# A hybrid decoder layer on one core: the attention phase laid out by an event loop, and its result sent to the output projection through DRAM

## The chip, the core and the metric

The kernel runs on one core of a Trainium2 chip. The metric is device microseconds for one execution. The engines have these names: PE is TensorE (matmuls and transposes), ACT is ScalarE, DVE is VectorE, POOL is GpSimd, and SP is SyncE, which here does nothing but issue DMAs. Each engine takes its instructions in the order in which they were written into its own queue, and waits at an instruction whose inputs or buffers are not ready.

## What is computed

The kernel is one decoder layer on x of shape (1, 2048, 1024), float32:

```python
h = rms_norm(x, norm1_g)
proj = h @ w_in
o_a = swa_sink_mixer(qa, ka, va, sinks, rel_bias)     # 4 heads, window 128
o_b = s5_mixer(u, ...)                                # state-space scan, 512 wide
o_c = nsa_mixer(qc, kvc, gates, ...)                  # 4 heads, three branches
mixed = concat([rms_norm(o_a, g), rms_norm(o_b, g), rms_norm(o_c, g)])
x = x + mixed @ w_out
hid = relu(rms_norm(x, norm2_g) @ w_up)
x = x + (hid * hid) @ w_down
```

Inside `nsa_mixer` each block of 128 query rows attends in three branches, and the gated sum of the three is the 256-wide row o_c:

```python
o_cmp = softmax(q @ k_cmp + bias) @ v_cmp     # up to 128 compressed keys ("c")
idx   = top_k(sums of p_cmp, 16)              # 64-row key blocks
o_sel = softmax(q @ k[idx] + bias) @ v[idx]   # selected blocks ("s")
o_win = softmax(q @ k[last 512] + bias) @ v   # window ("w")
o = g0 * o_cmp + g1 * o_sel + g2 * o_win
```

The kernel does not gather the selected blocks. It takes logits against all keys up to the diagonal and adds a mask through extra rows of the key and query tiles.

## The kernel before

Every matmul operand is split into a high and a low part, so that one product is three matmuls: `mm3` (L74) issues high by high (L76), high row by low weight (L77) and low row by high weight (L78). The phases follow one another in the program: the input projection, then attention A, the scan's output and the compression merged together, then `phase_mix` (L978), then the up projection and the down projection. This text is about `phase_mix`: attention C for 16 blocks of 128 rows and the output projection of each.

**One block of attention.** `prep` (L1049) loads the block's q, k and v rows into `tc`, makes the doubled rows `qd` on POOL, transposes them on PE (tiles `ptqc`, `ptkc`, L793) and splits them into `qA`/`qB` and the key tiles. For each branch and each of four heads `Attn.logits` (L827) multiplies q with up to 512 keys at a time into a PSUM tile (`pqc`, `pqw`, `pqs`; L843/L844; two buffers). DVE adds the bias and takes the running maximum (L846), and ACT takes the exponential (L851) into the probabilities `slc`, `slw`, `sls`. `Attn.pv` (L854) then goes over the probabilities two key blocks at a time, for a pair of heads. PE transposes four 128 by 128 pieces into a PSUM tile (`ppc`, `ppw`, `pps`; L864; two buffers). ACT casts this tile to the high part (`thc`, `thw`, `ths`; L867), DVE subtracts that from it to get the low part (`tlc`, `tlw`, `tls`; L868), and PE multiplies both with the values (L872) into `poc`, `pow` or `pos`. I call one such tile a probability tile; a run of the phase has 260 of them (32 of c, 84 of w, 144 of s). `Attn.combine` (L876) copies the branch's result (`oT`), transposes it back (`ptoc`, `ptow`, `ptos`, L884), scales it by the gate on DVE (`ot`) and adds it on POOL into `oc` (L888, L891; three buffers).

**The projection of one block.** `finish_steps` (L1191) loads the rows of A and B into `mix`, scales them on POOL, takes ACT's square (L897) and POOL's reciprocal root of `oc`, and writes the scaled `oc` into the last quarter of `mix` (L899). PE transposes `mix` in two halves (`ptx`, L1212), ACT and DVE split them (`mh` L1214, `ml` L1215), and 48 matmuls with 512 columns (`pw`, L76 to L78) form the 128 by 1024 result. DVE adds the input rows `mx` (L1227), ACT squares (L1230) and sends the rows to DRAM. For blocks 0 to 7 the rows are also scaled (L1239), transposed (`pth`, L1247) and stored in `hT`; for the later blocks `mt` reads rows of `hT` back and `block_sums` (L1260) makes differences that go to `sums` in DRAM. The up projection reads `hT` and `sums` as its factors `fx` (L1431) and splits them on ACT (L1345) and DVE (L1346) into `fh` and `fl`; its first matmuls are `pua` (L1499).

**What sets the order.** `phase_mix` makes lists of steps: the probability products of one pair of heads, the logits of the next, the preparation of the next block, and the projection of the block before. `merge` (L68) interleaves them evenly by their numbers of steps. Within this the framework's scheduler may shift instructions by priority. The projection's matmuls are given low priority (`FILL = 500`, and for blocks 13 to 15 the numbers of `ENDS`), so that they fill gaps of PE; the products with the values may lag by `LAG = 30`, and the transposes of `combine` by `LAG_TURN = 10`.

Of the kernel before, what the change touches and what calls it, by code (L numbers as in the profile page):

```python
# [16 lines left out]
P = 128  # L17
D = 1024
# [10 lines left out]
FILL = 500  # L29
ENDS = {13: 1, 14: 1000, 15: 1000}  # L30
LAG = 30
LAG_TURN = 10
# [942 lines left out]
RING = 6  # L975


def phase_mix(tc, C, x, gains, B, cmp, w_out, out_norm_g, g2, pd, oa_d, ob, x1, hT, xs, rr, rh, ss_a, ss_b, r_d, release):  # L978
    nc = tc.nc
    kcA, kcB, vc = cmp  # L980
    with ExitStack() as ctx:
# [9 lines left out]
        A = Attn(tc, C, lp, sm, ps_s, ps_p, ps_o, ps_t, LAG)  # L991
        small = A.small
# [14 lines left out]
        late = {}  # L1007

        def open_late():
# [19 lines left out]
            nc.sync.dma_start(rt, r_d.rearrange("(i p) -> i p", p=P))  # L1029
            pt = late["ps"].tile([P, NT], F32, tag="pw", name="ptr")  # L1030
            nc.tensor.transpose(pt, rt, C["ident"][:NT, :NT])
            rb = fp.tile([P, NT], F32, name="r_b")
            nc.vector.tensor_copy(rb, pt)
            late["ra"], late["rb"] = ra, rb
            for k in range(NK):
                load_wout(k)

        def load_wout(k):
            fp, wh, wl, go = (late[n] for n in ("fp", "wh", "wl", "go"))
            for n in range(2):  # L1040
                sl = slice(512 * n, 512 * n + 512)
                if n == 0:
                    raw_k = fp.tile([P, D], F32, tag="xt", name=f"oraw{k}", bufs=2)
                    nc.sync.dma_start(raw_k, w_out[0, k * P:(k + 1) * P])
                raw = raw_k[:, sl]
                nc.scalar.activation(wh[k][:, sl], raw, AF.Copy, scale=go[:, k:k + 1])
                nc.vector.scalar_tensor_tensor(wl[k][:, sl], raw, go[:, k:k + 1], wh[k][:, sl], op0=ALU.mult, op1=ALU.subtract)

        def prep(i):  # L1049
            tcc = lp.tile([P, 524], F32, tag="tc", name=f"tc{i}", bufs=1)  # L1050
            nc.sync.dma_start(tcc[:, 0:256], pd["b"][i * P:i * P + P, 128:384])
            nc.sync.dma_start(tcc[:, 256:524], pd["c"][i * P:i * P + P, 128:396])
            qd = lp.tile([P, 6, 2, 64], F32, tag="qd", name=f"qdc{i}", bufs=1)
            twice(nc, qd[:, 0:4], tcc[:, 0:256].rearrange("p (h d) -> p h d", d=64), rh[:, i, 0:4])
            twice(nc, qd[:, 4:6], tcc[:, 256:512].rearrange("p (h d) -> p h d", d=P)[:, :, 0:64], rh[:, i, 4:6])
            pt = turn(nc, C, ps_t, qd, 0, 4, f"qc{i}")
            qA = lp.tile([P, 4, P], F32R, tag="qA", name=f"qA{i}")
            qB = q_lo[i % 2]
            split_q(nc, qA, qB, pt, gains[:, 2:3])
            pt = turn(nc, C, ps_t, qd, 4, 2, f"kc{i}")  # L1060
            ks, kw = slice(i * P, i * P + P), slice((i % RING) * P, (i % RING) * P + P)
            split_k(nc, kAs[:, ks], pt[:, 0], gains[:, 4:5])
            split_k(nc, kAw[:, kw], pt[:, 1], gains[:, 5:6])
            nc.vector.tensor_copy(kBs[0:64, ks], kAs[0:64, ks])
            nc.vector.tensor_copy(kBw[0:64, kw], kAw[0:64, kw])
            vw[i] = lp.tile([P, P], F32R, tag="vw", name=f"vw{i}", bufs=6)
            split_v(nc, Vs[:, i], tcc[:, 320:384])
            split_v(nc, vw[i], tcc[:, 448:512])
            gt = small(12, "gt")
            nc.scalar.activation(gt, tcc[:, 512:524], AF.Tanh, scale=0.5)  # L1070
            nc.vector.tensor_scalar(gt, gt, 0.5, 0.5, op0=ALU.mult, op1=ALU.add)
            return qA, qB, gt.rearrange("p (h b) -> p h b", b=3)

        def cmp_steps(i, qA, qB, gt, oc):
            n = 8 * (i + 1)
            box = {}
            nm, den, w = small(4, "nmc"), small(4, "denc"), small(4, "wc")

            box["sl"] = slc

            def slab():
                return slc

            def po():
                if "po" not in box:
                    box["po"] = ps_o.tile([P, 512], F32, tag="po", name=f"poc{i}")
                return box["po"]
            res = []
            for h in range(4):
                res += A.logits(lambda h=h: slab()[:, h], h, qA, qB, [(0, B["cmp"][:, h, 120 - 8 * i:P], [(kcA[:, 0:n], kcB[:, 0:n])])], -NEG, nm, den, f"c{i}")  # L1090

            def recip():
                nc.vector.reciprocal(den, den)
                if i == 0:
                    nc.vector.tensor_scalar(den, den, C["rows31"], None, op0=ALU.mult)
                nc.vector.tensor_tensor(w, den, gt[:, :, 0], op=ALU.mult)
            res.append(recip)

            def select():
                sl = box["sl"]  # L1100
                nb = 2 * (i + 1)
                pn = lp.tile([P, 4, P], F32, tag="qd", name=f"pn{i}", bufs=1)
                pm = late["fp"].tile([P, P], F32, tag="pm", name=f"pm{i}", bufs=1)
                nc.gpsimd.tensor_tensor(pn[:, :, 0:n], sl[:, :, 0:n], den.unsqueeze(2).broadcast_to([P, 4, n]), op=ALU.mult)
                nc.vector.tensor_reduce(pm[:, 0:n], pn[:, :, 0:n].rearrange("p h m -> p m h"), axis=AX.X, op=ALU.add)
                im, s2, m8 = small(32, "im", 1), small(32, "s2", 1), small(8, "m8", 1)
                nc.vector.tensor_reduce(im[:, 0:nb], pm[:, 0:n].rearrange("p (j f) -> p j f", f=4), axis=AX.X, op=ALU.add)
                nc.vector.tensor_tensor(im[:, 1:nb], im[:, 1:nb], pm[:, 3:n - 1:4], op=ALU.add)
                nc.vector.tensor_tensor(im[:, 0:nb], im[:, 0:nb], C["forced"][:, 30 - 2 * i:30 - 2 * i + nb], op=ALU.max)
                nc.vector.memset(im[:, 0:1], 1e4)  # L1110
                nc.vector.max(m8, im[:, 0:nb])
                nc.vector.match_replace(s2[:, 0:nb], m8, im[:, 0:nb], NEG)
                nc.vector.max(m8, s2[:, 0:nb])
                nc.vector.match_replace(s2[:, 0:nb], m8, s2[:, 0:nb], NEG)
                mk = C["mk"]
                nc.vector.tensor_scalar(mk[:, 64:64 + nb], s2[:, 0:nb], NEG, 1.0, op0=ALU.is_equal, op1=ALU.subtract)
                pt = ps_t.tile([P, 4, P], F32, tag="pt", name=f"ptm{i}")
                nc.tensor.transpose(pt[0:96, 0], mk, C["ident"])
                nc.vector.tensor_copy(qB[64:96], pt[64:96, 0:1].broadcast_to([32, 4, P]))
            for pair in range(2):  # L1120
                res += A.pv(lambda pair=pair: po()[:, 256 * pair:256 * pair + 256], lambda pair=pair: [box["sl"][:, 2 * pair], box["sl"][:, 2 * pair + 1]],
                            lambda b: vc, 1, f"c{i}{pair}")
            res.append(lambda: A.combine(po(), w, oc, True, f"c{i}"))
            if i >= 8:
                res.append(select)
            return res

        def units(i, qA, qB, gt, oc):

# [758 lines left out]
```

## Time and profile before

| | us |
| --- | --- |
| median of 3 runs | 2563.53 (2557.38 to 2566.71) |
| the profiled execution, its own time | 2563.24 |
| span of the profiled execution | 2561.4 |
| mean granted clock of PE, share of full | 0.988 |
| PE busy | 2460.4 |
| DVE busy | 1788.2 |
| ACT busy | 1329.7 |
| POOL busy | 1025.0 |

The times run from the start of the span. Attention C begins at about 612 us, when the last work of the state-space branch still runs beside it; from 712 us it runs with the projection alone; the last product with the values ends at 1278 us, and the first matmul of the up projection starts at 1303.2 us. So `phase_mix` takes some 690 us of the 2561. A matmul's record in the trace reaches from its start to its modelled end, and neighbouring records overlap: one with 512 columns is 0.39 us long where the next starts 0.23 us after it. The busy time of PE therefore counts the ends of matmuls as work, and short waits vanish in it. "Dense" in this text means the time that matmuls need when they follow one another without any wait.

### The profile page before, as it was taken

The page shows a single profiled execution, that of the slowest core. Times are in us where ns is not written, and L with a number is a line of the kernel's source. Part 1 is how long each engine was busy: PE and PEld are TensorE (multiplying, and loading weights), DVE is VectorE, ACT ScalarE, POOL GpSimd, SP SyncE. Part 2 cuts the span into 40 slices and gives each one's busy share as a digit, 9 for nine tenths or more (in the row PEclk, how much of TensorE's full clock was granted, in tenths as well). Part 3 has the DMA queues.
Part 4 walks back from the last instruction along what each step waited for, and adds up shares of the span by engine and source line. Part 5 has one row for each costly group of instructions (what it writes and reads, how often), then busy time and mean ns, then how long its engine had stood idle before and what let it go on. Part 6 is the DMA issues. An engine that isn't in the chain of part 4 may idle for free.

```text
span 2561.4 us, 38083 instructions
## 1 busy us (share of the span) xinstructions
PE 2460.4 (96%) x12766; PEld 2065.3 (81%) x12766; DVE 1788.2 (70%) x3496; ACT 1329.7 (52%) x2768; POOL 1025.0 (40%) x1015
## 2 busy tenths in 40 slices
PE   8999998999899999999989999999999999999999
PEld 8899997777778777778768888788887888888887
DVE  7853876754766677788565655655557888888886
ACT  6453546755766665565455554544444444344442
POOL 0000222212333333242366666566545344544447
PEclk9999999999899999999999999999999999999999
DMA  7462326221312112121456667655547534444336
GB/s 233 136 203 82 108 93 177 75 57 52 112 48 71 58 57 83 44 83 41 148 179 200 186 183 228 211 167 146 151 126 256 165 97 133 133 132 128 120 103 197
DMA packets 390261, 333.02 MB, mean 130 GB/s; under 512 B 42247, under 2 KB 353165, under 8 KB 388625
## 3 DMA queue, kind: packets, MB, share of 16 engines
q1 hardware_dynamic: 352880, 304.37, 39.5%
q10 hardware_dynamic: 37184, 26.22, 3.2%
q8 instruction: 101, 1.65, 0.3%
q14 instruction: 96, 0.78, 0.1%
HBM read 218.05 MB, written 112.45 MB: 129 GB/s over the span
## 4 chain that ended last, share of the span: by engine, by line
PE 63%; DVE 4%; ACT 3%; issue 2%; POOL 2%; DMA 2%; SPq 0%; DVEq 0%; POOLq 0%; ACTq 0%
PE pdc L1678 7%; PE pdb L1678 7%; PE pda L1678 7%; PE pub L1499 6%; PE puc L1499 6%; PE pua L1499 6%; PE pdd L1678 3%; PE pud L1499 3%; PE pos L872 2%; PE pps L864 2%; PE pw L76 2%; PE pw L77 2%; PE pw L78 2%; PE pqs L843 1%; DVE sls L846 1%
## 5 line engine op out<-in xcount | busy, mean ns | idle before, releaser
L1345 ACT CAST v<-vr 128x512 fp32r<-128x512 f32 x224 | 139.4, 624 | 303.6 <-DMA vr<-vd 138.5
L1346 DVE TENSOR_TENSOR v<-vr,v 128x512 fp32r<-128x512 f32 x224 | 235.5, 1059 | 78.9 <-ACT v L1345 77.0
L1678 PE MATMUL pdc<-dw,v 128*128 128x512 f32 x768 | 187.5, 393 | 4.3 <-ACT dw L1345 4.3
L1678 PE MATMUL pdb<-dw,v 128*128 128x512 f32 x768 | 184.9, 390 | 0.0
L1678 PE MATMUL pda<-dw,v 128*128 128x512 f32 x768 | 184.5, 389 | 0.0
L1678 PEld LDWEIGHTS pdc<-dw,v 128*128 128x128 f32 x768 | 145.5, 190 | 35.7 <-ACT dw L1345 4.7
L1678 PEld LDWEIGHTS pdb<-dw,v 128*128 128x128 f32 x768 | 144.6, 188 | 30.2
L1678 PEld LDWEIGHTS pda<-dw,v 128*128 128x128 f32 x768 | 144.1, 188 | 30.0
L550 POOL TENSOR_TENSOR t<-Q,E 128x508 f32<-128x508 f32 x16 | 22.0, 1374 | 364.0 <-ACT Q L530 325.8
L1470 POOL TENSOR_TENSOR fs<-ur,ur 128x512 f32<-128x512 f32 x62 | 92.1, 1485 | 160.3 <-DMA ur<-in_w_up 127.5
L1345 ACT CAST uh<-fs 128x512 fp32r<-128x512 f32 x124 | 76.2, 621 | 151.2 <-PE pub L1499 59.7
L1346 DVE TENSOR_TENSOR ul<-fs,uh 128x512 fp32r<-128x512 f32 x124 | 128.1, 1034 | 32.5 <-ACT uh L1345 32.4
L1346 DVE TENSOR_TENSOR ul<-ur,uh 128x512 fp32r<-128x512 f32 x93 | 101.0, 1087 | 48.9 <-ACT uh L1345 43.1
L76 PE MATMUL pw<-wo_h,mh 128*128 128x512 f32 x256 | 110.2, 431 | 4.3 <-DVE ml L1215 2.0
L868 DVE TENSOR_TENSOR tls<-pps,ths 128x512 fp32r<-128x512 f32 (+1 forms) x144 | 92.9, 658 | 29.8 <-ACT ths L867 22.5
L1515 POOL TENSOR_TENSOR ev<-e,e 128x512 f32<-128x512 f32 x64 | 92.2, 1440 | 47.4 <-issue 25.2
L867 ACT CAST ths<-pps 128x512 fp32r<-128x512 f32 (+1 forms) x144 | 79.1, 565 | 57.8 <-PE pps L864 27.5
L1499 PE MATMUL pub<-fh,uh 128*128 128x512 f32 x256 | 102.5, 401 | 2.9 <-DVE e L1508 2.9
L77 PE MATMUL pw<-wo_l,mh 128*128 128x512 f32 x256 | 104.9, 410 | 0.0
L78 PE MATMUL pw<-wo_h,ml 128*128 128x512 f32 x256 | 104.5, 409 | 0.0
L1499 PE MATMUL pub<-fl,uh 128*128 128x512 f32 x256 | 102.0, 398 | 0.1
L1499 PE MATMUL puc<-fh,uh 128*128 128x512 f32 x256 | 101.1, 395 | 0.9 <-DVE eu L1508 0.9
(563 smaller groups left out, 7855.9 us busy)
## 6 DMA issues: line engine op xcount, KB each, us to landing
vr<-vd SPq DMA_DIRECT2D x224, 256.0 KB
vd<-ev SPq DMA_DIRECT2D x128, 256.0 KB
ur<-in_w_up SPq DMA_DIRECT2D x124, 256.0 KB
vd<-e ACTq DMA_DIRECT2D x64, 256.0 KB
dr<-in_w_down SPq DMA_DIRECT2D x32, 512.0 KB
x<-in_x SPq DMA_DIRECT2D x16, 512.0 KB
mx<-in_x SPq DMA_DIRECT2D x16, 512.0 KB
x<-mx ACTq DMA_DIRECT2D x16, 512.0 KB
```

The lines of the kernel that those rows point to most:

```text
L76: nc.tensor.matmul(out, sh, mh, start=first, stop=False)
L77: nc.tensor.matmul(out, sh, ml, start=False, stop=False)
L78: nc.tensor.matmul(out, sl, mh, start=False, stop=last)
L864: nc.tensor.transpose(pt[:, j, hh], sls[hh][:, (b0 + j) * P:(b0 + j + 1) * P], C["ident"])
L867: nc.scalar.copy(th[:, 0:nb], pt[:, 0:nb])
L868: nc.vector.tensor_tensor(tl[:, 0:nb], pt[:, 0:nb], th[:, 0:nb], op=ALU.subtract)
L1345: nc.scalar.copy(dh, src)
L1346: nc.vector.tensor_tensor(dl, src, dh, op=ALU.subtract)
L1470: nc.gpsimd.tensor_tensor(t, x, y, op=op)
L1499: nc.tensor.matmul(bank[b], w[:, k], h[o][:, k], start=first and k == 0 and n == 0, stop=k == HALF - 1 and n == 2, skip_group_check=True)
L1515: nc.gpsimd.tensor_tensor(tile_("v" + o), x, y, op=op)
L1678: nc.tensor.matmul(bank[b, q], x[:, q, j], y[:, j], start=first and j == 0 and n == 0, stop=j == 1 and n == 2, skip_group_check=True)
```

## The change

The constants `FILL`, `ENDS`, `LAG` and `LAG_TURN` go. `phase_mix` is written anew as routines (Python generators), one or more for each stage of each block: `front`, `keys`, `values`, `compressed`, `select`, `attended`, `logits`, `reduced`, `turned`, `split_p`, `products`, `combined`, `finished`, `filled`, `added`, `posted`. A routine yields an event that it waits for, a ring of buffers that it needs a place in, or an operation as (engine, nanoseconds, function). While the program is built, an event loop (`Flow.run`) keeps the time of each engine, picks the operation that could start first, with the routine's rank deciding among equals, writes its instructions, and moves the engine's time on. All of it stands in `tc.manual_schedule()`, so that the order written is the order on the engines. The rank is 100 times the block number plus an offset.

```diff
-FILL = 500
-ENDS = {13: 1, 14: 1000, 15: 1000}
-LAG = 30
-LAG_TURN = 10
+    def start(self, task):
+        e = task.op[0]
+        t = max(task.t + HEARD[e], self.engines[e])
+        return t if task.engine in (None, e) else max(t, task.end + HEARD[e])
+
+    def run(self):
+        while self.ready:
+            task = min(self.ready, key=lambda k: (self.start(k), k.rank, k.number))
+            s, (e, ns, fn) = self.start(task), task.op
+            self.ready.remove(task)
+            fn()
+            self.engines[e] = s + max(ns - EARLY[e], 30)
+            task.engine, task.end = e, s + ns + TOLD[e]
+            self.advance(task, task.end)
...
+def mm_ns(n):
+    return 8 + 0.427 * n
...
+def cast_ns(n):
+    return 197 + 0.72 * n
...
+            yield "ACT", cast_ns(n), lambda: nc.scalar.copy(th[:, 0:nb], pt[:, 0:nb])
...
+            spawn(products(th, tl, hi, lo, nb, b0, nblk, v_of, name, po_of, prev, me, finished), rank - 1)
+            t = yield "DVE", sub_ns(n), lambda: nc.vector.tensor_tensor(tl[:, 0:nb], pt[:, 0:nb], th[:, 0:nb], op=ALU.subtract)
...
+                t = yield "SP", 50, lambda: nc.sync.dma_start(oc_d[i * P:i * P + P], S["oc"].rearrange("p h d -> p (h d)"))
...
+            rank, fill = 100 * i + R_FINISH, 100 * i + (BACKLOG if i < ENDING else R_FINISH)
...
+                nc.sync.dma_start(mix[:, 768:D], oc_d[rows])
...
+            yield "ACT", 630, lambda: nc.scalar.activation(sq, dst, AF.Square, accum_out=ss)
...
+                for m, (a, b) in enumerate(((mh, wh), (mh, wl), (ml, wh))):
+                    t = yield "PE", mm_ns(512), lambda: nc.tensor.matmul(pw[n], a[half][:, j], b[k][:, sl], start=k == 0 and m == 0, stop=k == NK - 1 and m == 2)
...
+BACKLOG = 400
+R_FRONT = -90
+R_CMP = -88
+R_SELECT = -30
+R_LOGITS = -20
+R_FINISH = 190
+ENDING = 14
```

The arithmetic stays. Both programs issue 12522 PE, 3482 DVE, 2501 ACT and 1020 POOL instructions. The one difference in the work is that `oc` of each block now goes to a DRAM tile `oc_d` and comes back into the last quarter of `mix`, in two DMAs of 128 KB per block (SP has 1259 instructions instead of 1227); `oc` has two buffers instead of three, and `mh` and `ml` are split into halves of their own. The transposes `ptx` and `pth` use the PSUM buffer that `combine` and the preparation use, instead of the one of `pw`. Outside `phase_mix` the code is the same.

On PE in the middle of the phase, before: a probability tile's products (`pos`), a transpose of the window branch (`ppw`) and projection matmuls stand singly among each other.

```order
4354 L76 MATMUL pw_10562<-wo_h_7678,mh_10459 128x512
4355 L77 MATMUL pw_10562<-wo_l_7679,mh_10459 128x512
4356 L78 MATMUL pw_10562<-wo_h_7678,ml_10460 128x512
4357 L872 MATMUL pos_11256<-ths_11527,Vs 128x256
4358 L872 MATMUL pos_11256<-tls_11528,Vs 128x256
4359 L76 MATMUL pw_10562<-wo_h_7680,mh_10459 128x512
4360 L864 MATMUL ppw_11589<-c_ident,slw_11444 128x128
4361 L77 MATMUL pw_10562<-wo_l_7681,mh_10459 128x512
4362 L78 MATMUL pw_10562<-wo_h_7680,ml_10460 128x512
4363 L76 MATMUL pw_10562<-wo_h_7682,mh_10459 128x512
4364 L77 MATMUL pw_10562<-wo_l_7683,mh_10459 128x512
4365 L864 MATMUL ppw_11589<-c_ident,slw_11514 128x128
```

On PE at the like place in the changed program, where L1296/L1297 are the logits, L1354 the products, L1321 the transposes of probabilities and L1657 the projection:

```order
4374 L1296 MATMUL pqs_11496<-kAs,qA_10835 128x512
4375 L1297 MATMUL pqs_11496<-kBs,qB_7329 128x512
4376 L1296 MATMUL pqs_11507<-kAs,qA_10835 128x512
4377 L1297 MATMUL pqs_11507<-kBs,qB_7329 128x512
4378 L1354 MATMUL pow_11380<-tlw_11466,vw_8630 128x256
4379 L1354 MATMUL pow_11380<-tlw_11466,vw_9135 128x256
4380 L1321 MATMUL ppw_11510<-c_ident,slw_11267 128x128
4381 L1321 MATMUL ppw_11510<-c_ident,slw_11270 128x128
4382 L1657 MATMUL pw_11369<-wo_h_7598,ml_11321 128x512
4383 L789 MATMUL ptkc_11536<-c_ident,qdc_11304 128x128 x2
4384 L1296 MATMUL pqs_11518<-kAs,qA_10835 128x512
4385 L1297 MATMUL pqs_11518<-kBs,qB_7329 128x512
4386 L1657 MATMUL pw_11369<-wo_h_7600,mh_11320 128x512
```

A tile's instructions now stand together, and a single projection matmul fills a place between them.

On PE at the end of the phase, before: the last products of attention, the back-transposes `ptow`, half of the transposes of block 15's `mix`, and then its projection.

```order
6144 L872 MATMUL pow_15620<-thw_15716,vw_14642 128x256
6145 L872 MATMUL pow_15620<-tlw_15717,vw_14642 128x256
6146 L884 MATMUL ptow_15744<-c_ident,oTw_15742 128x128 x4
6147 L1212 MATMUL ptx_15783<-c_ident,mix_15753 128x128 x2
6148 L76 MATMUL pw_15794<-wo_h_7678,mh_15774 128x512
```

On PE at the end of the phase now: the last projection matmuls of block 14, all eight transposes of block 15's `mix` (`ptx`), and its projection; the last instruction of attention (`ptow`) is row 5946, and what stands between it and row 6050 is projection.

```order
6048 L1657 MATMUL pw_15791<-wo_l_7609,mh_15709 128x512
6049 L1657 MATMUL pw_15791<-wo_h_7608,ml_15710 128x512
6050 L1622 MATMUL ptx_15807<-c_ident,mix_15726 128x128 x4
6051 L1622 MATMUL ptx_15840<-c_ident,mix_15726 128x128 x4
6052 L1657 MATMUL pw_15860<-wo_h_7594,mh_15805 128x512
6053 L1657 MATMUL pw_15860<-wo_l_7595,mh_15805 128x512
6054 L1657 MATMUL pw_15860<-wo_h_7594,ml_15806 128x512
```

In the changed program 148 projection matmuls follow the last instruction of attention, where 48 did before.

On SP at the end of the phase, before: a load of an up factor (`fx<-sums`, row 495) stands ahead of the last load of input rows.

```order
489 L1258 DMA mt_15456<-hT 128x2x128 x4
490 L1198 DMA mix_15753<-oa_d 128x256
491 L1431 DMA fx_15917<-hT 128x2048
492 L1265 DMA sums<-mt_15456 128x2x128 x4
493 L1199 DMA mix_15753<-ob 128x512
494 L1458 DMA ur_15925<-in_w_up 128x4x128
495 L1431 DMA fx_15919<-sums 128x2048
496 L1201 DMA mx_15756<-in_x 128x1024
```

On SP at the end of the phase now: the writes to `sums` of blocks 13 and 14 (rows 539 and 542), and behind them the loads of factors.

```order
536 L1597 DMA mix_15726<-oc_d 128x256
537 L1638 DMA mx_15721<-in_x 128x1024
538 L1715 DMA mt_15741<-hT 128x2x128 x4
539 L1720 DMA sums<-mt_15741 128x2x128 x4
540 L1638 DMA mx_15837<-in_x 128x1024
541 L1715 DMA mt_15857<-hT 128x2x128 x4
542 L1720 DMA sums<-mt_15857 128x2x128 x4
543 L1852 DMA fx_16003<-sums 128x2048
544 L1852 DMA fx_16053<-sums 128x2048
```

The buffers of `mt` and `mx` are the same two (`xt`), so that `mt` of block 14 (row 541) waits until an earlier block's rows have left theirs.

More of the change, by code (lines that the diff above doesn't have):

```diff
@@ L975, with __init__ @@
 RING = 6
-def phase_mix(tc, C, x, gains, B, cmp, w_out, out_norm_g, g2, pd, oa_d, ob, x1, hT, xs, rr, rh, ss_a, ss_b, r_d, release):
+EARLY = {"PE": 0, "ACT": 98, "DVE": 78, "POOL": 43, "SP": 0}
+TOLD = {"PE": 177, "ACT": 9, "DVE": 12, "POOL": 10, "SP": 0}
+HEARD = {"PE": 103, "ACT": 22, "DVE": 22, "POOL": 68, "SP": 30}
+class Event:
+    def __init__(self):
+        self.time, self.waiting = None, []
+class Ring:
+    def __init__(self, n):
+        self.free, self.waiting = [0.0] * n, []
+class Task:
+    def __init__(self, gen, rank, number, t):
+        self.gen, self.rank, self.number, self.t = gen, rank, number, t
+        self.op = self.engine = None
+        self.end = 0.0
@@ L1029, in open_late, with turn_rows @@
             nc.sync.dma_start(rt, r_d.rearrange("(i p) -> i p", p=P))
+            late["ra"], late["rt"] = ra, rt
+        def turn_rows():
             pt = late["ps"].tile([P, NT], F32, tag="pw", name="ptr")
[L1031 to L1034, printed above, removed]
-            for k in range(NK):
[L1036 to L1047, printed above, removed]
@@ L1092, in recip @@
+            po, half = po_box(f"poc{i}")
+            fin = [{n: Event() for n in ("turned", "split", "pv")} for _ in range(2)]
+            for e in exps:
+                yield e
+            yield ev["gt"]
             def recip():
@@ L1095, in recip @@
                     nc.vector.tensor_scalar(den, den, C["rows31"], None, op0=ALU.mult)
[L1096 to L1106, printed above, removed]
+                nc.vector.tensor_tensor(w, den, S["gt"][:, :, 0], op=ALU.mult)
@@ new lines, in added @@
+        def added(i, n, pw, x_, landed, done, alt):
+            S = T[i]
+            yield landed
+            xt = x_[:, 512 * n:512 * n + 512]
+            if "xs" not in S:
+                S["xs"] = small(2, "xs")
+            ss = S["xs"]
+            yield "DVE", 683, lambda: nc.vector.tensor_tensor(xt, xt, pw, op=ALU.add)
+            t = yield "ACT", 789, lambda: nc.scalar.activation(pw, xt, AF.Square, accum_out=ss[:, n:n + 1])
+            put(R["pt" if alt else "pw"], t)
+            fire(done, t)
@@ L1783, in trunk @@
         r_d = dr.tile([L], F32, name="r_d")
+        oc_d = dr.tile([L, 256], F32, name="oc_d")
         c_all = ctx
@@ L1811, in trunk @@
             run(merge(swa, glu, b_nsa + c_steps))
[L1812 removed]
+        phase_mix(tc, C, x, gains, B, cmp, w_out, out_norm_g, norm2_g, pd, oa_d, ob, x1, hT, sums, rr, rh_c, ss_a, ss_b, r_d, oc_d, c_u.close)
         c_b.close()
```

705 lines of the change are left out of this document (520 added, 185 removed).

## The prediction

> **What bounds the kernel now.** I read the page's first part, then the windows, then PE's groups of lines, PE's timeline, and the waits.
>
> From the page, the span and the engines' busy times:
>
> ```profile
> span 2561.4 us, 38083 instructions
> PE 2460.4 (96%) x12766; PEld 2065.3 (81%) x12766; DVE 1788.2 (70%) x3496; ACT 1329.7 (52%) x2768; POOL 1025.0 (40%) x1015
> ```
>
> The windows of the phase that changes, and last a window of the down projection for comparison (start:end, length, busy time and count of each engine, granted clock, DMA share, GB/s):
>
> ```profile
> 612.00:712.00 100.00, 89.29 (x490) 71.36 (x488) 77.56 (x270) 69.56 (x216) 33.48 (x53) 0.90 0.28 88
> 712.00:1262.00 550.00, 518.26 (x3217) 431.21 (x3216) 397.37 (x1143) 331.66 (x777) 177.67 (x392) 0.99 0.20 63
> 1262.00:1306.00 44.00, 34.54 (x152) 27.19 (x151) 21.45 (x23) 15.73 (x28) 28.70 (x37) 0.88 0.64 204
> 1162.00:1262.00 100.00, 97.59 (x599) 81.13 (x598) 71.95 (x183) 57.45 (x112) 27.52 (x66) 1.00 0.20 63
> 2000.00:2100.00 100.00, 100.00 (x443) 82.81 (x442) 83.28 (x98) 45.52 (x70) 43.44 (x23) 1.00 0.40 116
> ```
>
> PE looks full in 712 to 1262: 518 of 550 us. It isn't. In the last window nothing waits, and 443 matmuls of 512 columns take 100 us, so one needs 0.226 us, 0.44 ns a column. For the smaller ones I take runs of one kind from PE's timeline:
>
> ```profile
> 901.05 0.40 PE L76 MATMUL pw<-wo_h,mh 128*128 128x512 f32 x1
> 902.19 0.55 PE L864 MATMUL pps<-c_ident,sls 128*128 128x128 f32 x3 [0.74 <-ACT sls L851]
> ...
> 906.54 0.40 PE L872 MATMUL pos<-tls,Vs 128*128 128x256 f32 x2
> 906.77 0.28 PE L872 MATMUL poc<-thc,vc 128*128 128x256 f32 x1
> ...
> 910.28 1.06 PE L864 MATMUL pps<-c_ident,sls 128*128 128x128 f32 x8
> ```
>
> Two products of 256 columns take 0.40, one 0.28, so one more costs 0.12. Eight transposes take 1.06; with 0.28 for the record of one, one more costs (1.06-0.28)/7 = 0.11. The first two rows show why busy time misleads: the transposes start 1.14 us after a matmul that needs 0.23, so 0.91 us are lost, of which the row shows 0.74 as idle.
>
> Now the dense time of 712 to 1262, by PE's groups in that window:
>
> ```profile
> L76 PE MATMUL pw<-wo_h,mh 128*128 128x512 f32 x214 | 91.1, 426 | 1.9 <-ACT pw L1230 0.9 <-DVE ml L1215 0.6
> L864 PE MATMUL pps<-c_ident,sls 128*128 128x128 f32 x514 | 87.1, 278 | 3.7 <-ACT sls L851 1.7 <-DVE s L1114 0.9 <-DVE tls L868 0.2
> L872 PE MATMUL pos<-ths,Vs 128*128 128x256 f32 x258 | 64.5, 309 | 1.6 <-ACT ths L867 1.4
> ...
> L843 PE MATMUL pqs<-kAs,qA 128*128 128x512 f32 (+3 forms) x144 | 58.4, 406 | 5.1 <-DVE mx L846 3.6 <-DVE nmc L846 0.7 <-DVE nms L846 0.3
> ...
> L864 PE MATMUL ppw<-c_ident,slw 128*128 128x128 f32 x228 | 44.2, 282 | 1.1 <-DVE tlw L868 0.5 <-ACT slw L851 0.3
> L843 PE MATMUL pqw<-kAw,qA 128*128 128x128 f32 (+2 forms) x118 | 36.1, 315 | 2.0 <-DVE nms L846 0.9 <-DVE nmw L846 0.7 <-DVE mx L846 0.4
> ...
> L872 PE MATMUL pow<-thw,vw 128*128 128x256 f32 x112 | 29.9, 311 | 0.2 <-ACT thw L867 0.2
> ```
>
> The projection has 643 matmuls (three lines, about 214 each): 145 us. Transposes of probabilities: 786 by 0.11 = 87. Products with the values (s, w and c, high and low): 786 by 0.117 = 92. Logits priced by their columns (pqs 2 by 144, pqw 2 by 118, pqc 2 by 44): 92. The other 390 transposes: 42. The sum is 458 us in 550, a density of 83%. The same count gives 67 of 100 for 612 to 712, 29 of 44 for 1262 to 1306, and 90 of 100 for 1162 to 1262. So the phase holds 554 us of work in 694, and 140 are lost.
>
> By the Trainium skill ("Trainium Kernel Development and Optimization", Performance Expectations), matmul busy time is a bad measure of how close a kernel is to its limit, because matmuls are pipelined. The trace agrees: 518 us busy, 458 of work.
>
> Where are the 92 us lost in the middle? PE's longest named waits there are small:
>
> ```profile
> PE pth L1247 <- POOL mx L1239: 7.3, 7, 1.9
> PE pqs L843 <- DVE mx L846: 3.6, 7, 1.0
> PE ppc L864 <- DVE tls L868: 3.4, 4, 1.1
> ```
>
> Most of it is in pieces of 0.1 to 1 us ahead of instructions that wait for ACT or DVE: a probability tile goes PE, ACT, DVE, PE, through two buffers, and each hand-off that comes late costs a little. DVE (397 of 550) and ACT (332) aren't full.
>
> **The change part by part.** The arithmetic is the same, instruction for instruction; only order, four buffers and a DRAM round trip change. So I price density.
>
> *Middle and end.* Dense work after 712: 458+29 = 487 us, in 594 now. The changed program leaves 148 projection matmuls and a few transposes behind attention, 148 by 0.226 + 2 to 3 = 36 us; the rest, 451 us, runs with attention. Two things decide its density. For it: the order is laid out with a time for each operation that fits the trace (227 ns for 512 columns, 566 for the cast, against 226 and 565 in the rows here), so that PE is seldom sent to a tile that isn't there, and single projection matmuls stand between (12.65 blocks' projections are done when the last selected branch of block 15 ends, against 14.5 before). Against it: between the last transpose of a tile and its first product now stands PE work of 1.46 us (median of the 260 tiles, counted in the order and priced as above) where 2.36 stood. The hand-off itself needs, by ACT's and DVE's groups over 612 to 1306,
>
> ```profile
> L867 ACT CAST ths<-pps 128x512 fp32r<-128x512 f32 (+1 forms) x144 | 79.1, 565 | 57.8 <-PE pps L864 27.5 <-PE pos L872 22.5 <-PE poc L872 2.5
> L868 DVE TENSOR_TENSOR tls<-pps,ths 128x512 fp32r<-128x512 f32 (+1 forms) x144 | 92.9, 658 | 29.8 <-ACT ths L867 22.5 <-PE pos L872 5.1 <-PE pw L78 0.4
> ```
>
> 0.57 us for the high part, 0.57+0.66 = 1.23 for the low one, so 1.46 covers the high part with 0.9 to spare for queueing on ACT. The bounds of density are 83% (as now) and 100%; the nearest row is the window 1162 to 1262, where projection matmuls were plentiful and density was 90%. I take 91%: 451/0.91 = 496 us. The tail of 36 us has no hand-offs but its own: 94%, 38.5 us. Together 534, so 594-534 = 60 us less. At 88% it would be 43 less, at 94% 76 less.
>
> *Start.* In 612 to 712, 33 us are lost, mostly beside the old branches' last work, which is unchanged. Weights are loaded in another order, but no earlier. I take 70% for 67%: 4 us less; bounds 0 and 10.
>
> *The round trip through DRAM.* Each block's `oc` goes out and in. The nearest row is a load in the chain of waits:
>
> ```profile
> 651.23 2.42 DMA tc<-pc
> 1258.28 3.81 DMA mt<-hT
> 1263.81 4.17 DMA sums<-mt
> ```
>
> Two of 2.4 to 4.2 us make 5 to 8 us of delay per block. Behind the waiting write and read on SP stand the next rows `mx`, a store of `hT` and the next block's `tc`. All of that is needed a block later (over 40 us), and PE has two blocks of projection in hand meanwhile; at the last block 100 matmuls of block 14, 22 us, cover it. I cost it at nothing; uncovered, it would be 16 times 5 to 8 = 80 to 128 us. A third buffer of `oc` is no longer needed, since the row leaves for DRAM at once.
>
> By the Trainium skill ("DMA: Bandwidth & Descriptors", Anatomy of one DMA), every DMA pays about 2 us however small. The trace's 2.42 us agrees; by that figure alone the round trip would be an estimated 4 us per block, 64 us if nothing hid it.
>
> *The exit.* Now PE idles before the projection of block 15, and then goes on without a wait into the up projection:
>
> ```profile
> 1284.53 0.39 PE L78 MATMUL pw<-wo_h,ml 128*128 128x512 f32 x1
> 1291.62 0.69 PE L1212 MATMUL ptx<-c_ident,mix 128*128 128x128 f32 x2 [6.70 <-POOL mix L899]
> ...
> 1294.00 0.63 PE L76 MATMUL pw<-wo_h,mh 128*128 128x512 f32 x1
> 1294.43 0.63 PE L77 MATMUL pw<-wo_l,mh 128*128 128x512 f32 x1
> ...
> 1303.20 0.39 PE L1499 MATMUL pua<-fh,uh 128*128 128x512 f32 x1
> ```
>
> After the 6.7 us idle, matmuls follow at 0.43 us instead of 0.23 for some 4 us (granted clock 0.88 in that window), about 2 us lost. This gap goes, and is in the 60 us. But a new one comes. The factor loads `fx<-sums` now stand behind the last differences on SP, and those wait until block 14's rows have left their buffer. The pieces:
>
> ```profile
> 1301.55 4.96 DMA fx<-sums
> 1306.58 1.92 ACT fh L1345
> 1308.52 2.30 DVE fl L1346
> ```
>
> and the window behind up's start as it is now:
>
> ```profile
> 1306.00:1331.00 25.00, 23.01 (x98) 17.67 (x97) 19.51 (x17) 17.44 (x21) 12.39 (x11) 1.00 0.78 247
> ```
>
> From the end of block 14's projection: add and square 1.3, x1 to DRAM 2.4, `mt` 3.8, differences on POOL 2.2, `sums` 4.2, `fx` 5.0, `fh` 1.9, `fl` 2.3: 23 us, with issues about 24. PE has in that time block 15's transposes, a wait of 2 for their split, 48 by 0.226 = 10.8, and up's first twelve matmuls 2.7: 16.2. Idle: 8 us, and 1.6 for the slow pace behind it, together 9.6, of which 25 - 98 by 0.226 = 2.9 are lost in that window already now: +7. Bounds 0 and 15.
>
> The Trainium skill ("TensorE: Matmul & The Clock Gate", Part 1) says that the clock halves after an idle window of about 3.4 us and returns after as long a busy one. The rows agree (6.70 us idle, then about 4 us at half pace); by its figure the new gap's price would be an estimated 1.7 us, and it speaks against the exit of this order.
>
> *The sum*, against the profiled execution's 2563.2 us (span 2561.4, 1.8 around it; the median 2563.53 is 0.3 more): -4 -60 +7 = -57, **2506 us**.
>
> **The rivals.**
>
> *No gain in density.* The order is better only by the planner's numbers; the losses come from jitter of ACT and DVE, and stay. 451/0.83 + 38.5 = 582, -12; with -4 and +7: 2554 us. For it: DVE must work 72% of the time now and 79% if the middle shrinks to 503 us, so its queue is longer. Against: the window at 90% has the same DVE load (72 of 100).
>
> *Slower: the shorter cover.* A fixed order with 1.46 us instead of 2.36 between transposes and products meets an ACT that is behind by more than 0.9 us, and every tile waits. ACT's exponential of a selected head lasts 1.2 us by its group,
>
> ```profile
> L851 ACT ACTIVATE sls<-sls,nms 128x128 f32<-128x128 f32 (+15 forms) x64 | 77.6, 1212 | 20.6 <-DVE nms L846 20.5
> ```
>
> and a cast behind one is late by up to that. If each of 260 tiles loses 0.2 us more, with density otherwise as now: 2554 + 52 = 2606 us. It makes the kernel slower than the 0.5% bound from 0.09 us a tile. Against it: there are 64 such exponentials to 260 tiles, and 0.9 us of the cover is left beside the cast.
>
> *A larger gain.* PE always finds work: 97%, 465 us, 2475 us. Against it: no window of this phase has come over 90%.
>
> **How the numbers follow.** Forecast 0.60 (88 to 94%: 2490 to 2523), no gain 0.12 (2554), slower 0.16 (2606), larger gain 0.12 (2475). The range takes in all but the slower case: 2470 to 2575. A measurement of this kernel tells about 0.5%, 13 us, from no change: faster is below 2550.7. The forecast, the larger gain and a quarter of the no-gain case make 0.75; the rest of that case is 0.09 the same; slower 0.16.
>
> **What would show it.** Right: attention's middle at over 88% dense, that is, the 3200 matmuls of 712 to 1262 done in some 60 us less; no wait on `mix` for `oc_d` in the middle; an idle of about 8 us on PE before up's second group; DVE busy near 79%. Wrong: long waits of products for `th` (the shorter cover), waits of `ptx` for POOL's `mix` (the round trip), or a middle as long as now.

## The result, and the profile after

The changed kernel takes 2548.28 us (median of 4 runs, 2548.03 to 2551.73); the kernel before took 2560.45 us beside it. The ratio is 0.9947, with a 95% interval of 0.9933 to 0.9961: 12 us faster, where 57 were forecast. The profiled execution has a span of 2546.6 us, 14.8 us less than before.

The span and the engines' busy times of the changed kernel:

```profile
span 2546.6 us, 37996 instructions
PE 2440.5 (96%) x12766; PEld 2071.8 (81%) x12766; DVE 1771.2 (70%) x3496; ACT 1325.9 (52%) x2768; POOL 1021.1 (40%) x1015
```

The windows of the phase after the change: its start in two halves, the middle, and the tail in two parts (columns as before):

```profile
612.00:662.00 50.00, 35.47 (x163) 28.55 (x164) 22.64 (x101) 18.61 (x67) 4.79 (x6) 0.85 0.11 27
662.00:712.00 50.00, 42.23 (x243) 35.07 (x242) 44.62 (x134) 39.55 (x116) 17.91 (x22) 0.88 0.28 90
712.00:1222.00 510.00, 498.09 (x3274) 437.58 (x3275) 407.64 (x1182) 338.54 (x806) 177.03 (x383) 1.00 0.25 77
1222.00:1262.00 40.00, 24.70 (x95) 19.18 (x95) 11.01 (x15) 9.19 (x22) 32.42 (x55) 0.83 0.45 141
1262.00:1300.00 38.00, 30.04 (x126) 23.49 (x125) 12.93 (x13) 12.56 (x17) 12.73 (x28) 0.91 0.63 202
```

The middle got what was forecast, and the ends gave most of it back. 3274 matmuls now take 510 us where 3217 took 550. Counting every matmul at its dense price, as the prediction did, gives the time lost on PE, stretch by stretch:

| stretch | lost before, us | lost after, us | change | forecast |
| --- | --- | --- | --- | --- |
| start, 612 to 712 | 33.2 | 46.4 | +13.2 | -4 |
| middle, 712 to the last matmul of attention (1279.6, 1221.1) | 94.5 | 47.2 | -47.3 | -50 |
| tail, from there to the first of up (1303.2, 1279.5) | 12.2 | 22.6 | +10.4 | -10 |
| exit, first to 1001st matmul of up: 241.9, 252.0 us long | | | +10.1 | +7 |
| the rest, to PE's last matmul: 1011.3, 1010.1 us long | | | -1.2 | 0 |

(The -60 forecast for middle and tail was 451/0.91 - 451 = 45 lost in the one and 2.5 in the other.) The sum is -14.8 us, the difference of the spans. The middle's density rose from 473.1 in 567.6 us, 83.4%, to 462.0 in 509.1, 90.7%.

The groups of probabilities and products in the middle of the changed kernel show where it came from; before, the waits ahead of `pps`, `ppw` and `pos<-ths` were 3.7, 1.1 and 1.6 us, and many more too short for such a column:

```profile
L1321 PE MATMUL pps<-c_ident,sls 128*128 128x128 f32 x520 | 77.0, 272 | 0.0
L1354 PE MATMUL pos<-ths,Vs 128*128 128x256 f32 x260 | 61.5, 314 | 0.0
L1296 PE MATMUL pqs<-kAs,qA 128*128 128x512 f32 (+3 forms) x145 | 57.8, 400 | 2.0 <-DVE nmw L1273 0.7 <-DVE mx L1273 0.6 <-DVE nms L1273 0.6
L1354 PE MATMUL pos<-tls,Vs 128*128 128x256 f32 x260 | 54.7, 288 | 1.7 <-DVE tls L1342 1.6
```

Products follow their casts without a wait, with the shorter cover. Most of the gain is in short pieces. I counted what a matmul comes later than its dense price, in 712 to 1262 before and 712 to 1212 after; the counts are rough, since they shift with the price given to each matmul. Pieces of 0.1 to 0.3 us fell from some 26 us in all to some 7, those of 0.3 to 1 us from some 26 to some 18, and longer ones from 14 (18 us) to 2 (3 us).

At the start, PE's timeline stands still for 8 us, and DVE's timeline tells why. First the last rows of PE ahead of the wait and the one behind it:

```profile
652.62 0.39 PE L74 MATMUL gpm<-glu_h,zl 128*128 128x512 f32 x1
652.84 0.39 PE L626 MATMUL gpm<-glu_bh,glu_ones 128*128 128x512 f32 x1
661.20 0.69 PE L1321 MATMUL ppc<-c_ident,slc 128*128 128x128 f32 x2 [7.96 <-DVE tls L1342]
```

and DVE over the same time:

```profile
634.01 0.17 DVE L40 TENSOR_SCALAR rah<-ss_a 128x16 f32<-128x16 f32 x1
635.15 0.69 DVE L634 SCALAR_TENSOR_TENSOR ga<-gb,gpm 128x512 f32<-128x512 f32 x1 [0.97 <-PE gpm L626]
...
645.30 0.69 DVE L634 SCALAR_TENSOR_TENSOR ga<-gb,gpm 128x512 f32<-128x512 f32 x1 [7.32 <-PE gpm L626]
653.33 0.69 DVE L634 SCALAR_TENSOR_TENSOR ga<-gb,gpm 128x512 f32<-128x512 f32 x1 [7.34 <-PE gpm L626]
653.93 0.17 DVE L41 TENSOR_SCALAR r_a<-rah 128x16 int32<-128x16 int32 x1
...
659.45 0.17 DVE L1139 TENSOR_SCALAR r_c<-r_c 128x16 f32<-128x16 f32 x1
```

DVE does nothing of attention from 634 to 659.7 us. `open_late` (the 28 small instructions of the reciprocal roots and a halving, `rah` to `r_c`) stands in one piece in its fixed order; its second instruction writes into memory that the gated unit of branch B (`gpm`, `ga`) releases, and stands behind that unit's last `ga`. Before, the same instructions came after the unit's last `ga` (652.91 us) and stood singly among those of attention:

```profile
655.19 0.17 DVE L44 TENSOR_SCALAR rah<-ss_b 128x16 f32<-128x16 f32 x1
655.28 0.18 DVE L846 CUSTOM_DVE_ANT_0 slc<-pqc,b_cmp 128x24 f32<-128x24 f32 x1
...
665.97 0.18 DVE L1026 TENSOR_SCALAR r_c<-r_c 128x16 f32<-128x16 f32 x1
```

In the tail, PE waits four times for the single `pw` buffer, three of them long, and runs at half pace behind two:

```profile
1225.36 0.51 PE L1657 MATMUL pw<-wo_h,mh 128*128 128x512 f32 x1 [2.89 <-ACT pw L1673]
...
1237.18 0.79 PE L1657 MATMUL pw<-wo_h,mh 128*128 128x512 f32 x1 [6.09 <-ACT pw L1673]
1237.77 0.63 PE L1657 MATMUL pw<-wo_l,mh 128*128 128x512 f32 x1
1238.20 0.63 PE L1657 MATMUL pw<-wo_h,ml 128*128 128x512 f32 x1
...
1257.71 0.79 PE L1657 MATMUL pw<-wo_h,mh 128*128 128x512 f32 x1 [5.02 <-ACT pw L1673]
```

The buffer is freed by DVE's add and ACT's square. At the first wait the add stands on DVE behind the split of a factor of the up projection (`fl`, 2.28 us). ACT's timeline ahead of the second wait:

```profile
1230.78 0.42 ACT L1608 ACTIVATE sq<-mix 128x256 f32<-128x256 f32 x1 [5.46 <-DMA mix<-oc_d]
1231.10 0.19 ACT L1608 ACTIVATION_READ_ACCUMULATOR sq<-mix 128x1 f32 x1
1231.19 0.60 ACT L1766 CAST uh<-ur 128x512 fp32r<-128x512 f32 x1
```

and DVE's:

```profile
1231.83 0.69 DVE L1767 TENSOR_TENSOR ul<-ur,uh 128x512 fp32r<-128x512 f32 x1 [6.67 <-ACT uh L1766]
...
1235.65 0.67 DVE L1672 TENSOR_TENSOR mx<-mx,pw 128x512 f32<-128x512 f32 x1
```

This is a chain through queues and not through data. ACT stands 5.46 us at the square of block 14's row, which is on its way back from DRAM. It comes late because of SP's queue: SP waits for POOL's last add before it can write block 15's row to DRAM (1226.49 us), and block 14's load (1227.85) stands behind that write.

```profile
SPq L1579 <- POOL oc L1399: 9.6, 1, 9.6
```

Seven casts of the up projection (`uh`) stand behind ACT's square, the up projection's subtractions (`ul`) wait for those on DVE, and the add that would free `pw` stands behind them, though its product is done at 1231. The third long wait is another: there the add most likely waits for its input rows, which SP issued at 1251.50 (the profile names the load issued right behind them, `mt<-hT`).

At the exit, as forecast, the up projection's second and third groups wait for factors:

```profile
1284.81 0.50 PE L1920 MATMUL pud<-fh,uh 128*128 128x512 f32 x1 [2.42 <-ACT fh L1766]
1288.74 0.80 PE L1920 MATMUL puc<-fh,uh 128*128 128x512 f32 x1 [3.42 <-ACT fh L1766]
```

### The profile page after: what moved, and what is told of

Read it like the earlier page. It is cut to its first block, busy times and chain, and to the rows that moved or that the text cites. A ratio compares the mean times of both kernels' runs of the same rounds, so it can differ in the third digit from the quotient of the medians.

```text
span 2546.6 us, 37996 instructions
## 1 busy us (share of the span) xinstructions
PE 2440.5 (96%) x12766; PEld 2071.8 (81%) x12766; DVE 1771.2 (70%) x3496; ACT 1325.9 (52%) x2768; POOL 1021.1 (40%) x1015
## 5 line engine op out<-in xcount | busy, mean ns | idle before, releaser
L1767 DVE TENSOR_TENSOR ul<-ur,uh 128x512 fp32r<-128x512 f32 x93 | 93.5, 1007 | 50.1 <-ACT uh L1766 46.8
L1657 PE MATMUL pw<-wo_h,mh 128*128 128x512 f32 x256 | 104.8, 409 | 16.5 <-ACT pw L1673 15.5
L1342 DVE TENSOR_TENSOR tls<-pps,ths 128x512 fp32r<-128x512 f32 (+1 forms) x144 | 92.5, 657 | 21.4 <-ACT ths L1337 20.2
L1657 PE MATMUL pw<-wo_h,ml 128*128 128x512 f32 x256 | 104.4, 408 | 0.0
L1657 PE MATMUL pw<-wo_l,mh 128*128 128x512 f32 x256 | 104.1, 407 | 0.0
```

The lines of the kernel that those rows point to most:

```text
L1342: t = yield "DVE", sub_ns(n), lambda: nc.vector.tensor_tensor(tl[:, 0:nb], pt[:, 0:nb], th[:, 0:nb], op=ALU.subtract)
L1657: t = yield "PE", mm_ns(512), lambda: nc.tensor.matmul(pw[n], a[half][:, j], b[k][:, sl], start=k == 0 and m == 0, stop=k == NK - 1 and m ...
L1767: nc.vector.tensor_tensor(dl, src, dh, op=ALU.subtract)
```

## The experiments

All times are medians of 4 to 10 runs; ratios are to the kernel before, run beside them. Its median was 2560 to 2564 us from one series to the next, so differences between experiments are good to a few us. "Lost" is counted as in the table, in one profiled execution of each kernel. Every edit lets the event loop lay out the whole phase anew, so that more than the named instruction can move.

**e1_direct: no trip through DRAM.**

```diff
-                t = yield "SP", 50, lambda: nc.sync.dma_start(oc_d[...], S["oc"]...)
...
-                nc.sync.dma_start(mix[:, 768:D], oc_d[rows])
...
-            yield "ACT", 630, lambda: nc.scalar.activation(sq, dst, AF.Square, accum_out=ss)
+            yield "ACT", 630, lambda: nc.scalar.activation(dst, flat, AF.Square, accum_out=ss)
```

(`flat` is the block's `oc`; the scaling reads it too, and `oc` has three buffers.)

> The changed kernel with one part undone: the attended rows are squared and scaled into the last quarter of mix straight from their tile (three buffers), without the trip through DRAM. Changed kernel: 2548.3 us. Theory: at the end of the phase ACT's square of block 14's row waits for the row to come back from DRAM (5.46 us idle), the up projection's casts stand behind it on ACT, the up projection's subtractions behind these on DVE, and the add that would free the one pw buffer behind those; so PE waits 6.09 us for pw and then runs at half pace. Without the trip this wait and its slow pace go: 6 to 8 us less, 2540 to 2542. Rival: the other waits of the tail (late input rows, the up projection's work ahead of the add) take its place: within 2 us of 2548. In the middle neither expects a change: the density there stays at 90 to 91%.

Measured: 2533.70 us, 0.987 (0.9845 to 0.9896). The tail loses 14.7 us instead of 22.6, the middle 41.9 instead of 47.2. PE's waits from 1190 us on have this first row:

```profile
PE pw L1655 <- ACT pw L1671: 6.4, 4, 3.4
```

It was 15.3 us for the changed kernel. So the trip and the two buffers that go with it cost 15 us, not nothing (20 us by the ratios; e13_oc3 below takes the two apart). The gain is larger than either theory gave, as the middle gained too.

**e2_open1: the opening one block later.**

```diff
-            yield E[0]["w1"]
+            yield E[1]["w1"]
             yield "DVE", 5000, open_late
```

> The changed kernel with the opening of the projection's tiles (and the reciprocal roots for the A and B rows on DVE) one block later. Theory: DVE's roots write into memory that the gated unit of branch B still holds, so from 634 to 660 us every DVE instruction of attention stands behind the end of that unit; opened a block later, attention and the unit overlap again. Then 612 to 712 holds about 64 us of dense work instead of 54, and the time falls by 8 to 13 us: 2535 to 2540. Rival: the unit's matmuls are simply serial at that place, whatever DVE does: within 2 us of 2548.

Measured: 2535.14 us, 0.9884 (0.9869 to 0.9899). The theory's total, but not its place alone: the start loses 41.3 us instead of 46.4, the middle 3 and the exit 4.6 less, the tail 1.3 more. One wait that is left at the start stands behind the piece itself, which DVE now runs from 656.6 to 662.5 us:

```profile
663.94 1.12 PE L1387 MATMUL ptow<-c_ident,oTw 128*128 128x128 f32 x4 [4.95 <-DVE kAw L1243]
```

**e3_quick: a plan with wrong times.**

```diff
             s, (e, ns, fn) = self.start(task), task.op
+            if e in ("ACT", "DVE"):
+                ns = 100
```

> The changed kernel with the event loop told that every operation of ACT and DVE takes 100 ns; same instructions, other order. Counted in the order, the median PE work between a tile's last transpose and its first high product is 0.90 us (1.46 in the changed kernel, 2.36 before), and 202 of 260 tiles have less than 1.25 us ahead of their low product (12 in the changed kernel, 5 before). Theory: what makes the middle dense is that the plan leaves every hand-off the time that ACT and DVE need; told wrong, the density of the middle falls to 75 to 82% from 90 to 91%, 50 to 90 us longer there, 2595 to 2640 in all. Rival: what helps is that filler stands singly and everything is greedy, not the times: density 88% or more, under 2565.

Measured: 2853.87 us, 1.1125 (1.1102 to 1.1148). The window of the middle, and PE's longest waits in it:

```profile
712.00:1512.00 800.00, 636.57 (x3247) 495.04 (x3247) 422.25 (x1197) 351.04 (x818) 178.02 (x387) 0.89 0.15 47
```

```profile
PE pps L1323 <- ACT sls L1282: 24.1, 23, 2.3
PE pow L1356 <- ACT thw L1339: 23.3, 26, 1.9
...
PE pos L1356 <- DVE tls L1344: 11.0, 46, 1.1
```

The same 460 us of work take 807: a density of 57%, with the granted clock at 0.89, so that part of the loss is slow pace. The rival falls; the theory had the sign right and the size too small. Single filler and a greedy order aren't enough: the times in the plan matter, and with 0.90 us of cover instead of 1.46 products do wait for their casts. All times of ACT and DVE were wrong at once here; what the cover alone costs, and how exact the times must be, isn't shown.

**e5_end8: less projection kept back.**

```diff
-ENDING = 14
+ENDING = 8
```

> The changed kernel with ENDING 8 instead of 14: from block 8 on the projection's matmuls rank ahead of later attention instead of being kept back. After the last instruction of attention stand 72 projection matmuls instead of 148. Theory: the tail loses time because there the projection alone must hand its single buffer through DVE and ACT, so a tail with half the matmuls loses half: 8 to 12 us less, if the middle keeps its 90%: 2536 to 2541. Rival: the matmuls kept back are what fills the middle; without them its density falls to 86% and costs 20 us, 2555 to 2565.

Measured: 2559.29 us, 0.9981 (0.9968 to 0.9994). The rival held: the middle's density falls to 87.5%. The tail has half the work and loses 19.1 us all the same, because the last row's way is now uncovered:

```profile
PE ptx L1622 <- POOL mix L1604: 10.1, 1, 10.1
PE ptx L1622 <- POOL mix L1610: 2.5, 1, 2.5
```

**e6_both: e1_direct and e2_open1 together.**

> The changed kernel with both of the parts that helped alone: attended rows straight into mix, and the opening one block later. Alone they took 14.6 and 13.1 us off 2548.3. Theory: they act at different places (tail and middle; start and exit), so the gains add: 2519 to 2523. Rival: part of both is the same time at the end, so that 2526 to 2531 is left.

Measured: 2524.33 us, 0.9854 (0.9835 to 0.9874). Between the two ranges: 24 of the 27.7 us. The start loses 41.8 us, the middle 39.8, the tail 10.4; the exit's gain of e2_open1 isn't there (253.7 us).

**e7_both2: the opening two blocks later** (`E[2]` in the line of e2_open1).

> As e6_both, with the opening two blocks later instead of one. Theory: 612 to 712 still loses 41 us with the opening one block later, where the kernel before loses 33, so more of the wait goes: 4 to 8 us less than e6_both. Rival: by one block later the gated unit has ended; two blocks later only delays the weights of the projection, the filler comes later, and it is 0 to 6 us more than e6_both.

Measured: 2532.13 us, 0.9883 (0.9868 to 0.9898), 8 us more than e6_both. The rival's sign held, with more than its price.

**e8_end12: e6_both with ENDING 12.**

> As e6_both, with ENDING 12 instead of 14, so that 72 projection matmuls instead of 144 are left behind attention. Theory: the tail of projection alone loses 14 to 20 us because its single buffer goes through DVE and ACT at each half block; half the matmuls, half the loss, and the middle still has filler from eleven blocks: 4 to 8 us less than e6_both. Rival, after ENDING 8 cost 11 us: what is taken from the tail is missing in the middle, 0 to 8 us more than e6_both.

Measured: 2516.41 us, 0.9822 (0.9807 to 0.9837), the fastest here. 7.9 us less is what the theory gave, but by luck: the tail loses 13.1 us instead of 10.4. The gain stands at the exit, 244.9 us instead of 253.7: there SP sends the last `sums` on their way at 1243 us instead of 1255, and PE's wait of 8.7 us for a factor is gone. What is left in the tail is block 15's own way from POOL:

```profile
1242.48 0.69 PE L1620 MATMUL ptx<-c_ident,mix 128*128 128x128 f32 x2 [6.99 <-POOL mix L1607]
```

**e9_early: e6_both with early input rows.**

```diff
-            yield R["fill"]
             yield R["xt"]
...
             t = yield "SP", 50, lambda: nc.sync.dma_start(xt_, x[0, rows])
+            yield R["fill"]
```

> As e6_both, with the input rows mx of a block loaded before its turn at the projection instead of at it. Theory: what still keeps pw waiting in the tail (6.4 us of waits with the rows straight into mix) is the add that waits for late input rows; loaded early, 3 to 6 us less than e6_both. Rival: it is the up projection's casts and subtractions ahead of the add on ACT and DVE; no change within 2 us.

Measured: 2529.50 us, 0.9874 (0.9859 to 0.9889): 5 us more. Neither the theory nor the rival held. PE's waits for `pw` fall only from 5.3 to 4.5 us; the middle loses 3 us more than in e6_both and the tail 4, and the exit is 3 us shorter (the longest wait for a factor is 6.7 us instead of 8.7). The add's wait for its rows was read from the changed kernel, but loading them early with two buffers doesn't get the time back. Early rows hold one of the two buffers longer; that this is the cause isn't shown, and three buffers weren't tried.

**e10_square: the trip kept, ACT's square taken from the tile.**

```diff
+                t2 = yield "ACT", 630, lambda: nc.scalar.activation(sq, S["oc"]..., AF.Square, accum_out=ss)
...
-            yield "ACT", 630, lambda: nc.scalar.activation(sq, dst, AF.Square, accum_out=ss)
+            yield ev["ss"]
```

> The changed kernel with the trip through DRAM kept, and one instruction of each block moved: ACT's square takes the attended rows from their tile when they are done, not from mix when they have come back. The scaling on POOL still waits for the trip. Theory: what the trip costs is ACT's queue, which stands still at the square while the row is under way, with casts and the add's square behind it; then most of the 14.6 us of e1_direct come back: 2535 to 2540. Rival: it is the delay of the row itself (two DMAs) ahead of the last blocks' transposes, or two buffers instead of three; then 2545 to 2549.

Measured: 2537.34 us, 0.9897 (0.988 to 0.9914). 11 of the 14.6 us come back with the trip still there: tail 18.2, exit 247.3; the middle gains nothing. ACT still stands at a square, now that of block 15's row, since POOL's add is late:

```profile
1230.33 0.42 ACT L1584 ACTIVATE sq<-oc 128x256 f32<-128x256 f32 x1 [7.96 <-POOL oc L1399]
```

But less is behind it: two casts of the up projection instead of seven stand between it and the square that frees `pw`, and PE waits 3.70 us there instead of 6.09.

**e11_roots: e8_end12 with the roots on POOL.**

```diff
-            rsqrt_into(nc, sm, ra, ss_a, 1.0 / 256, NT, "ra")
+            rsqrt_into(nc, sm, ra, ss_a, 1.0 / 256, NT, "ra", nc.gpsimd)
```

(likewise for `rc` and its halving)

> As e8_end12 (2516.4 us), with the 28 small instructions of the reciprocal roots for the A and B rows on POOL instead of DVE. Theory: with the opening a block later PE still waits 4.95 us at 664 us for DVE, which runs the roots in one piece (28 of 0.2 us); on POOL they stand in nobody's way: 4 to 7 us less, 2509 to 2513. Rival: attention waits there for POOL's doubling of the query rows instead: within 2 us of 2516, or above.

Measured: 2523.64 us, 0.9841 (0.9826 to 0.9857), 7 us more than e8_end12 (5 us by the ratios). The wait for DVE behind the roots (4.95 us in e2_open1, 4.32 in e8_end12) is gone, and the start loses 42.3 us as before. It is the rival, and PE's timeline shows it: attention now waits for the doubled query rows, whose instruction stands behind the roots on POOL.

```profile
674.57 1.11 PE L789 MATMUL ptqc<-c_ident,qdc 128*128 128x128 f32 x4 [8.45 <-POOL qdc L782]
```

No stretch shows where the rest of the loss is.

**e12_roots0: the same with the opening at block 0.**

> As e11_roots, but with the opening at block 0 as in the changed kernel. Theory: the first root written into the memory of the gated unit waits for the unit's end on whatever engine it stands; on POOL only the doubling of query rows and the adds of attended rows stand behind it, not the logits and the low parts, so that 612 to 712 loses less than the 46 us with the roots on DVE but more than e11_roots: 2513 to 2522. Rival: POOL's queue blocks attention as much as DVE's did: 2524 to 2530.

Measured: 2527.76 us, 0.9859 (0.9841 to 0.9876), in the rival's range; the start loses 46.1 us, as with the roots on DVE. It shows what the opening waits for, though. POOL's timeline and then PE's:

```profile
630.62 0.20 POOL L40 TENSOR_SCALAR rah<-ss_a 128x16 f32<-128x16 f32 x1
645.45 0.20 POOL L41 TENSOR_SCALAR r_a<-rah 128x16 int32<-128x16 int32 x1 [14.63 <-DMA ob<-ga]
```

```profile
663.76 1.12 PE L789 MATMUL ptqc<-c_ident,qdc 128*128 128x128 f32 x4 [13.04 <-POOL qdc L782]
```

`r_a`, the second instruction of the piece, waits 14.63 us for a store of the unit (`ob<-ga`, the last but one) to leave the memory that it writes. The second root then waits 3.12 us for the unit's last square. This time the query rows stand behind the piece, and PE waits 13 us for them.

**e13_oc3: the changed kernel with three buffers for the rows.**

> The changed kernel with three buffers for the attended rows instead of two, the trip through DRAM kept. Without the trip (and with three buffers) the middle lost 42 us instead of 47 and the tail 15 instead of 23. Theory: both come from the trip; a third buffer alone does nothing, within 2 us of 2548. Rival: the 5 us of the middle come from compressed attention waiting for a free buffer while a row is under way to DRAM; then 2541 to 2545, with the gain in 712 to 1221.

Measured: 2545.96 us, 0.9933 (0.9916 to 0.995). The intervals of this and of the changed kernel overlap, and the middle loses 51.3 us and not less. So the third buffer is not what e1_direct gained in the middle. By the edits this kernel and e1_direct differ in the trip alone: it costs 12 us (16 by the ratios). The two profiled executions are 6 us apart: without the trip the middle loses 9 us less (41.9 against 51.3) and the tail 3 less, and the exit is 3 us longer. By which of the trip's effects the middle loses its part stays open.

This run shows one thing more, in PE's waits from 1195 us on:

```profile
PE pw L1657 <- ACT pw L1673: 8.3, 3, 6.1
```

The wait of 6.09 us behind block 14's square is gone with the trip still there: in this order SP loads block 14's row (1229.52 us) ahead of the write of block 15's (1233.30), and ACT squares for `pw` first (1235.19) and block 14's row after it (1235.82). The tail loses about 18 us and the exit is 247.1 us long, as in e10_square. So the chain in the tail hangs on where the plan puts the waiting instructions in the queues of SP and ACT, and e10_square can't give the price of one instruction alone.

## Why the prediction was wrong

The sign was right; the size was four to five times the measured one (57 us against 12, or 14.8 by the spans). By its own steps:

- **The middle: right.** 91% was taken, 90.7% came, with DVE busy 408 of 510 us, 80% (79 forecast). 45 us lost were forecast, 47.2 measured. The reason given, that the plan's times fit, is borne out by e3_quick as far as it goes: with times that are far off the density is lost.
- **The tail: failed.** "The tail of 36 us has no hand-offs but its own: 94%." It had 35.7 us of work as counted, and lost 22.6 us, not 2.5. The step missed two things. Its own hand-off is the single `pw` buffer, freed at every half block by an add and a square, and a tail without attention has nothing else to do meanwhile. And the queues of ACT and DVE hold the up projection's first work there.
- **The round trip at nothing: failed, for this reason.** The working asked what PE has in hand while the row is away, and on SP what stands behind its DMAs. But its list left out the block before: block 14's load stands behind block 15's write. And it didn't ask who stands behind the instruction that waits for the row on ACT. The cover was counted wrong too: of "100 matmuls of block 14, 22 us", only 48 are block 14's, since a block has 48, and all of them themselves needed ACT and DVE. The sign that the prediction named, waits of `ptx` for POOL's `mix`, didn't show; PE waited for `pw` instead. e1_direct against e13_oc3 gives 12 to 16 us for the trip. The queues of SP, ACT and DVE are how it reaches PE in the tail (9.6 us on SP, 5.46 on ACT, 6.09 on PE); the larger part is in the middle, and how it comes about there is open.
- **The start: failed.** "Weights are loaded in another order, but no earlier", -4 us. It came out +13.2. Not the weights but the opening moved: it now stands at block 0, in one piece and in a fixed order, ahead of attention on DVE. The order of DVE shows it; the working followed PE and SP alone. e2_open1 returns 13 us in all, 5 of them in this window. The window still loses 8 us more than before; part of it is the piece that stands undivided (waits of 4 to 5 us behind it on DVE, 8.45 on POOL), and the rest is open.
- **The exit: right in kind.** +7 was forecast, +10.1 measured, with two waits of 2.4 and 3.4 us for factors and a slow pace behind the second. e8_end12 makes it 9 us shorter than e6_both, with the last `sums` sent 12 us earlier.

Together the misses are +17 (start), about +20 (tail), +3 (middle) and +2 (exit and rest): 42 us, and 2506 + 42 = 2548.

Of the rivals, "no gain in density" gave 2554 us, near the measured time by its number and wrong in its mechanism: density did rise. "Slower, the shorter cover" fell for this order; its waits for `th` appear in e3_quick, at 0.90 us of cover and with all times of ACT and DVE wrong. The larger gain's density of 97% was not seen; 92.5% (e8_end12) was the highest.

The two parts that helped and a smaller backlog make 2516.41 us, 1.8% less than the kernel before and 1.25% less than the change as made (2516.41 against 2548.28, each against its own runs of before 0.9822 and 0.9947).

## What to carry to other kernels

A plan that gives each hand-off its measured time raised the density of a stage with many short dependences by 7 points here; a plan whose times were far off cost much more than the coarse order before did. But an engine takes its instructions in order, so that every wait is a wait of all that stands behind it. So for each instruction that waits for something far away (a DMA, memory that another phase releases) look at its own engine's queue: who is behind, and who waits for those. And price the ends of a stage apart from its middle: what hides a delay in the middle is missing where the work runs out.

## What the runs showed of the hardware

A POOL instruction beside DVE's long two-input subtractions took two to four times its usual time. The scaling of the two parts of `mix` took 1.44 and 1.64 us at 1233 us, beside DVE's subtractions of `ul`, and 0.48 and 0.70 us at 1257. The add of a row into `oc` has a mean of 0.74 us before; here it took 2.70 us while DVE split a factor:

```profile
1221.67 2.28 DVE L1767 TENSOR_TENSOR fl<-fx,fh 128x2048 fp32r<-128x2048 f32 x1
```

```profile
1221.84 2.70 POOL L1399 TENSOR_TENSOR oc<-oc,otw 128x256 f32<-128x256 f32 x1 [2.25 <-DVE otw L1392]
```

The Trainium skill ("GPSIMD Engine Reference", in its table of specifications) says that GpSimd shares its SBUF interfaces with VectorE and contends with instructions that read two inputs from there; these two rows agree (the profile's spans on POOL are rough). No run here took the two apart.
